# Sharing one pass over the index-query columns between the two halves of 64 tokens

## The chip, the cores and the metric

The kernel runs on one core of one Trainium2 chip. Its time is the device time of one execution in microseconds (us); a lower time is better. The core has a matrix engine (TensorE, PE in the rows; its weight loads are PEld), a vector engine (VectorE, DVE), a scalar engine (ScalarE, ACT), GpSimd (POOL) and a queue engine (SyncE, SP), which issues the transfers from memory here.

## The reference, cut to what matters

One decoder layer on 256 tokens with a model width of 4096. A modulated RMS norm makes `h`, one large projection makes `z`, and two head groups read parts of `z`:

```
mod = silu(c) @ w_ada + b_ada
shift, scale, gate = split(mod, 3)
h = rms_norm(x, norm_g) * (1 + scale) + shift          # 256 x 4096
z = h @ w_in                                           # 4096 x 15520, float32
uA, vA, gA, qB, kB, vB, gB, qI, kI, wI = split(z)
...
dots  = einsum('bqhd,bsd->bqhs', qI, kI)               # lightning indexer, 32 heads of 128
score = einsum('bqh,bqhs->bqs', wI, relu(dots))
score = where(s <= t, score, -inf)
_, sel = top_k(score, 64)                              # k_sel = SEQ / 4
...                                                    # attention over the selected keys
y = concat([yA, yB]) @ w_out
out = x + gate * y
```

`qI` takes 4096 of the 15520 columns of `w_in`, `kI` and `wI` together 160. A query at token t below 64 has at most 64 causal keys, so the top 64 take all of them whatever its scores are: its index queries need not be known.

## The kernel before, in words

**Float32 from three products.** A float32 matrix is split into a rounded part and a rest (`whi` and `wlo` for the weights, `hh` and `hl` for `h`), and `h @ w` is the sum of three products: `hh` with `whi`, `hl` with `whi` and `hh` with `wlo`. ACT writes `whi` (L408), DVE (L414) and POOL (L416) share `wlo`, and PE multiplies in `multiply` (L419 to L437, the matmul at L435). The 128x128 piece of `h` is the stationary operand and a piece of the weights of up to 512 columns streams past it.

**Tiles and blocks.** The unit of the stream is a tile: two rows of 128 of the contraction by up to 512 columns of weights, one transfer of 512 KB. Both token halves (n = 0 for tokens 0 to 127, n = 1 for 128 to 255) are multiplied with it, so a tile has 2 x 3 x 2 = 12 matmuls. The contraction (32 rows of 128) is cut into eight blocks of four. In each block all column groups of the list `early` are visited, two tiles each, and what comes out is added to the groups' sums in SBUF (`add_to`, L800 in the first block, L802 later). That is 46 tiles a block and 368 in all; 128 tiles of the gate columns and 128 of `w_out` follow, 624 in all.

**The head of a block.** The columns of `qI` and of `kI`, `wI` (names `qi0` to `qi7` and `kw`) come first in each block. The 160 columns of `kw` and the 512 of `qi7` are cut as two visits of 336 columns; seven visits of 512 columns follow. These 18 tiles (4 of 336 columns and 14 of 512) are called the head of the block below, the other 28 tiles its tail.

**What runs beside it.** During blocks 0 to 6 the next block's `shift` and `scale` are made on DVE from `w_ada`: 32 steps a block (L196), each with a transfer of 512 KB into one of two buffers `wa`; a step's program asks for the transfer after next (L178). `pace` spreads these steps evenly over the tiles. SP issues all transfers in the order of the program; `raw`, the buffer of a tile's weights, has four places, and a tile's transfer is asked for three tiles ahead (`AHEAD`). `make_h` then makes `hh` and `hl` of the next block, with the float32 `ht` in the pool `s2` (three places). In the last block there are no such transfers; from its eighth tile on the indexer runs between the tiles (`turn` and `weigh`: float32 transposes of `qi` with a reversing matrix `flip`, and float32 products with the keys).

The functions that the change touches and what calls them:

Of the kernel before, what the change touches and what calls it, by code (L numbers as in the profile page):

```python
# [15 lines left out]
P = 128  # L16
# [26 lines left out]
def layer(ctx, tc, x, c, w_ada, b_ada, norm_g, w_in, ln_v_g, ln_v_b, w_s, b_s, q_norm_g,  # L43
# [233 lines left out]
    def modulate(b, md, j, dst):  # L277

        for i in (j, j + 1):
            nc.scalar.activation(dst[:, i - j], xT[b][:, i], AF.Identity, scale=md[:, 1, i:i + 1],  # L280
                                 bias=md[:, 0, i:i + 1])

    def keep_h(b, hh, hl):
        for j in range(BLOCKS[b]):
            h_hi[starts[b] + j] = hh[:, j]
            h_lo[starts[b] + j] = hl[:, j]

    def first_h():
# [26 lines left out]
    def make_h(b, accs):  # L315
# [18 lines left out]
        for j in range(0, nk, 2):  # L334
            nc.gpsimd.tensor_sub(hl[:, j], hts[j // 2][:, 0], hh[:, j].bitcast(F32))
            nc.vector.tensor_sub(hl[:, j + 1], hts[j // 2][:, 1], hh[:, j + 1].bitcast(F32))
            if j + 2 == nk:
                keep_h(b, hh, hl)
            yield
# [40 lines left out]

    def visit(src, parts, ks, c0, w, read, soon=False, before=None):
        v = dict(src=src, parts=parts, ks=ks, c0=c0, w=w, read=read, soon=soon, before=before)
        visits.append(v)
        for i in range(0, len(ks), 2):
            stream.append((v, i))
# [33 lines left out]
    def multiply(t):  # L419

        v, i = stream[t]
        hi, lo = halves.pop(t)
        if i == 0:
            v["ps"] = [mm.tile([P, 512], F32, name="mm_ps", tag="mm") for _ in range(NT)]
        (ah, al), w, n_k = v["parts"], v["w"], len(v["ks"])
        nk = len(hi)
        todo = [(part, kk, n) for kk in range(nk) for part in range(2) for n in range(NT)]
        todo += [(2, kk, n) for kk in range(nk) for n in range(NT)]
        if t + 1 == len(stream):
            todo.sort(key=lambda x: x[2])  # L430
        for part, kk, n in todo:
            k = v["ks"][i + kk]
            a = al if part == 1 else ah
            b = lo if part == 2 else hi
            nc.tensor.matmul(v["ps"][n][:, :w], a[k][:, n * P:(n + 1) * P], b[kk][:, :w],  # L435
                             start=(i + kk == 0 and part == 0),
                             stop=(i + kk == n_k - 1 and part == 2))  # L437

    reads = []

    def step(t):
        load_w(t + AHEAD)
        due = [v for u, v in reads if u <= t]
        del reads[:len(due)]
        for v in due:
            if v["soon"]:
                v["read"](v["ps"])
        split(t)
        flush()
        for v in due:  # L450
            if not v["soon"]:
                v["read"](v["ps"])
        v, i = stream[t]
# [14 lines left out]

    groups["qi7"] = zp.tile([P, NT, 512], F32, name="qi7", tag="qi7")
    groups["kw"] = zp.tile([P, NT, 160], F32, name="kw", tag="kw")  # L470
# [19 lines left out]
    def indexer():  # L490
# [37 lines left out]
        def turn(g, n):  # L528
            tp = misc()
            for hh in range(4):  # L530
                nc.tensor.transpose(tp[:, hh * P:(hh + 1) * P], groups[f"qi{g}"][:, n, hh * P:(hh + 1) * P],
                                    flip)
            box = []

            def read():
                box.append(s2.tile([P, 512], F32, name="qit", tag="s2"))
                nc.scalar.activation(box[0], tp, AF.Copy)
            after(read)
            return box

        def weigh(g, n, qt):
            S = P * (n + 1)
            per = 512 // S
            for h0 in range(0, 4, per):
                dots = misc()
                for a in range(per):
                    nc.tensor.matmul(dots[:, a * S:(a + 1) * S], qt[:, (h0 + a) * P:(h0 + a + 1) * P],
                                     kiT[:, :S], start=True, stop=True)

                def read(dots=dots, h0=h0):  # L550
                    r = s2.tile([P, 512], F32, name="rel", tag="s2")
                    nc.scalar.activation(r, dots, AF.Relu)
                    for a in range(per):
                        hd = g * 4 + h0 + a
                        ws = wi[:, n, hd:hd + 1]
                        if hd == 28:
                            nc.vector.tensor_scalar(score[n], r[:, :S], ws, None, op0=OP.mult)
                        else:
                            nc.vector.scalar_tensor_tensor(score[n], r[:, a * S:(a + 1) * S], ws, score[n],
                                                           op0=OP.mult, op1=OP.add)  # L560
                after(read)

        for g in [7] + list(range(7)):
            for n in range(NT):
# [22 lines left out]
    def attend():  # L587
        mask, score = ix["mask"], ix["score"]

        def choose():  # L590
            for n in range(NT):
                S = P * (n + 1)
                sc = score[n]
                m = mask[:, :P] if n == 0 else mask[:, P:]
                nc.gpsimd.affine_select(sc, sc, pattern=[[-1, S]], compare_op=OP.is_ge, fill=FILL,
                                        base=n * P + P - 1, channel_multiplier=-1)
                yield
                mx = small([P, 8], f"mx{n}")
# [7 lines left out]
                yield  # L606
                nc.gpsimd.affine_select(m, m, pattern=[[-1, S]], compare_op=OP.is_ge, fill=NEG,
                                        base=n * P + P - 1, channel_multiplier=-1)
# [197 lines left out]
    for b, nk in enumerate(BLOCKS):  # L806
        for c0, w, parts in early:
            visit(w_in_t, (h_hi, h_lo), list(range(starts[b], starts[b] + nk)), c0, w, add_to(parts, b == 0),
                  soon=0 < b and nk == 2)
    n_early = len(stream)  # L810


    def mix(g):
# [12 lines left out]
        after(lambda: nc.vector.tensor_mul(wT, tp.rearrange("p (h t) -> p h t", h=4),  # L826
                                           keep[:, None, :].to_broadcast([P, 4, P])))
        yield
        for h0 in range(0, 4, 2):
# [77 lines left out]
    def make_gate(i):  # L907
# [7 lines left out]
        nc.vector.tensor_add(fl[0:1], fl[0:1], ada_tiles.pop(0)[0:1, 0, 0])  # L915
        load_ada()
        for a in range(2):
            hi = s2.tile([P, 512], F32R, name="ghi", tag="s2")
# [13 lines left out]

    GATE_STEPS = 4 * 36

# [142 lines left out]
```

## Time and profile before

| | |
|---|---|
| time, median of 3 runs | 1887.4 us (1884.28 to 1892.18) |
| the profiled execution | 1888.63 us, span from first to last instruction 1886.9 us |
| mean granted TensorE clock | 0.996 |
| PE busy | 1824.8 us, 97% of the span |
| DVE busy | 1447.4 us, 77% |
| POOL busy | 1295.3 us, 69% |
| ACT busy | 933.8 us, 49% |
| moved by transfers | 542.58 MB, mean 288 GB/s |

Busy time is the time in which an engine had at least one instruction under way. PE's matmuls overlap, so its busy share says that it nearly always had one, not how fast they went; the pace is read from the distance of starts. The DMA share is the time that packets took on the core's 16 DMA engines, as a share of their time; it can come out a little over 1.00 in a short stretch.

### The profile page before, as it was taken

To read this page: it belongs to the slowest core of one execution; us is meant where nothing else is said; L and a number is where in the kernel's file an instruction comes from. 1 tells how busy PE (TensorE), PEld (TensorE's weight loads), DVE (VectorE), ACT (ScalarE), POOL (GpSimd) and SP (SyncE) were. 2 spreads that over 40 slices of the span, in tenths; PEclk is the share of its full clock that TensorE was granted. 3 is DMA by queue.
4 is the path that set the end of the run, shared out by engine and by line. 5 is a ranking of instruction groups with operands and counts; after the bars stand their busy time and mean duration, and the time that the engine had idled before them with its cause. 6 is when DMAs were issued, how large, how long until landed. Compare 5 with 4: busy or idle time off the path is not lost. (4 is left out here: it accounts for less than half of the span.)

```text
span 1886.9 us, 27998 instructions
## 1 busy us (share of the span) xinstructions
PE 1824.8 (97%) x8324; PEld 1490.3 (79%) x8324; DVE 1447.4 (77%) x1762; ACT 933.8 (49%) x1737; POOL 1295.3 (69%) x1339
## 2 busy tenths in 40 slices
PE   5799999999999999999999999999999999999998
PEld 2487878878888888788888777787888888888887
DVE  4666888888888888888777898877777677677754
ACT  4356545344453454444445556566654554444443
POOL 0366777777777777777675546766567777877786
PEclk9899999999999999999999999999999999999999
DMA  9999998999989989999874477876789799899964
GB/s 311 339 338 340 332 322 304 331 316 306 335 304 322 321 300 324 328 309 340 284 207 146 128 224 262 272 257 202 242 281 312 248 323 338 295 307 350 334 212 156
DMA packets 269554, 542.58 MB, mean 288 GB/s; under 512 B 17270, under 2 KB 29784, under 8 KB 269404
## 3 DMA queue, kind: packets, MB, share of 16 engines
q1 hardware_dynamic: 269404, 540.79, 84.6%
q8 instruction: 68, 1.11, 0.2%
q14 instruction: 82, 0.67, 0.1%
HBM read 536.51 MB, written 4.22 MB: 287 GB/s over the span
## 5 line engine op out<-in xcount | busy, mean ns | idle before, releaser
L416 POOL TENSOR_TENSOR wlo<-raw,whi 128x512 fp32r<-128x512 f32 (+1 forms) x1248 | 1220.3, 1004 | 536.9 <-ACT whi L408 448.2
L408 ACT ACTIVATE whi<-raw 128x512 fp32r<-128x512 f32 (+1 forms) x1248 | 730.9, 619 | 834.9 <-DMA raw<-in_w_in_dram 407.5
L414 DVE TENSOR_TENSOR wlo<-raw,whi 128x320 fp32r<-128x320 f32 (+2 forms) x624 | 640.7, 1028 | 323.2 <-ACT whi L408 209.4
L435 PE MATMUL mm_ps<-whi,hh 128*128 128x512 f32 (+1 forms) x1984 | 620.4, 394 | 11.4 <-ACT whi L408 9.4
L435 PE MATMUL mm_ps<-whi,hl 128*128 128x512 f32 (+1 forms) x1984 | 604.9, 386 | 2.4 <-DVE hl L303 2.4
L435 PE MATMUL mm_ps<-wlo,hh 128*128 128x512 f32 (+1 forms) x1984 | 525.4, 386 | 5.7 <-DVE wlo L414 4.1
L196 DVE SCALAR_TENSOR_TENSOR acc<-wa,csil,acc 128x1024 f32<-128x1024 f32 x341 | 436.3, 1279 | 57.1 <-DMA wa<-in_w_ada_dram 56.4
L435 PEld LDWEIGHTS mm_ps<-wlo,hh 128*128 128x128 f32 x1984 | 368.9, 188 | 83.8 <-POOL wlo L416 8.8
L435 PEld LDWEIGHTS mm_ps<-whi,hh 128*128 128x128 f32 x1984 | 363.5, 189 | 90.2 <-ACT whi L408 19.9
L435 PEld LDWEIGHTS mm_ps<-whi,hl 128*128 128x128 f32 x1984 | 371.2, 188 | 77.3 <-DVE hl L303 2.9
L435 PE MATMUL mm_ps<-whi,yh 128*128 128x512 f32 x512 | 158.2, 390 | 0.0
L435 PE MATMUL mm_ps<-whi,yl 128*128 128x512 f32 x512 | 158.0, 389 | 0.0
L435 PE MATMUL mm_ps<-wlo,yh 128*128 128x512 f32 x512 | 137.5, 390 | 0.2
L435 PEld LDWEIGHTS mm_ps<-wlo,yh 128*128 128x128 f32 x512 | 95.9, 188 | 21.2 <-POOL wlo L416 1.5
L435 PEld LDWEIGHTS mm_ps<-whi,yh 128*128 128x128 f32 x512 | 95.9, 188 | 20.4 <-ACT whi L408 0.4
L435 PEld LDWEIGHTS mm_ps<-whi,yl 128*128 128x128 f32 x512 | 96.1, 188 | 20.0
L802 DVE TENSOR_TENSOR qi<-qi,mm_ps 128x512 f32<-128x512 f32 (+2 forms) x126 | 73.2, 616 | 0.0
L217 PE MATMUL acc<-wa,csil 128*1 128x512 f32 x64 | 28.1, 629 | 13.2 <-DMA wa<-in_w_ada_dram 13.2
L802 DVE TENSOR_TENSOR u<-u,mm_ps 128x512 f32<-128x512 f32 x56 | 35.6, 675 | 0.0
L802 DVE TENSOR_TENSOR v<-v,mm_ps 128x512 f32<-128x512 f32 x56 | 35.6, 675 | 0.0
L802 DVE TENSOR_TENSOR q<-q,mm_ps 128x512 f32<-128x512 f32 x56 | 35.6, 675 | 0.0
L222 DVE SCALAR_TENSOR_TENSOR accs<-wa,csil,accs 128x1024 f32<-128x1024 f32 x15 | 19.2, 1283 | 17.9 <-DMA wa<-in_w_ada_dram 17.8
(173 smaller groups left out, 797.2 us busy)
## 6 DMA issues: line engine op xcount, KB each, us to landing
raw<-in_w_in_dram SPq DMA_DIRECT2D x464, 512.0 KB, 5.9
wa<-in_w_ada_dram SPq DMA_DIRECT2D x384, 512.0 KB, 5.1
raw<-in_w_out_dram SPq DMA_DIRECT2D x128, 512.0 KB, 6.0
raw<-in_w_in_dram SPq DMA_DIRECT2D x32, 336.0 KB, 4.8
xs<-in_x_dram SPq DMA_DIRECT2D x8, 512.0 KB, 5.4
xres<-in_x_dram SPq DMA_DIRECT2D x8, 512.0 KB, 6.8
out_dram<-yt SPq DMA_DIRECT2D x16, 256.0 KB, 3.6
wk<-rb_d SPq DMA_DIRECT2D x16, 128.0 KB, 4.7
```

The lines of the kernel that those rows point to most:

```text
L196: nc.vector.scalar_tensor_tensor(dst, src, csil[:, k:k + 1], dst, op0=OP.mult, op1=OP.add)
L217: nc.tensor.matmul(acc[g:g + 1, s, :w], csil[:, k:k + 1], wt[:, s], start=i < 4, stop=i >= KC // 2 - 4)
L222: nc.vector.scalar_tensor_tensor(accs, wt, csil[:, k:k + 1], accs, op0=OP.mult, op1=OP.add)
L408: nc.scalar.activation(hi[kk][:, :w], raw[:, kk, :w], AF.Copy)
L414: nc.vector.tensor_sub(lo[kk][:, :cut], raw[:, kk, :cut], hi[kk][:, :cut].bitcast(F32))
L416: nc.gpsimd.tensor_sub(lo[kk][:, cut:w], raw[:, kk, cut:w], hi[kk][:, cut:w].bitcast(F32))
L435: nc.tensor.matmul(v["ps"][n][:, :w], a[k][:, n * P:(n + 1) * P], b[kk][:, :w], start=(i + kk == 0 and part == 0), stop=(i + kk == n_k - 1 ...
L802: nc.vector.tensor_add(z, z, p)
```

## The change

For the columns of `qI` the two halves of `h` of tokens 64 to 127 are laid side by side as one stationary operand of 128 columns (`both`: 64 tokens of the rounded part, 64 of the rest), and tokens 0 to 63 are left out. For n = 0 such a tile needs two products (`both` with `whi`, `both` with `wlo`) in place of three; it also takes along the product of rest with rest. A packed tile so has 10 matmuls in place of 12. The two halves of the sum are added later, in `turn`, by a product with `fold`, which reverses and adds in one (a float32 matmul of 64 columns in place of a transpose of 128). `weigh` and `choose` then work on 64 rows for n = 0. Visits of `kw` stay unpacked, since keys of all tokens are needed: so the 160 columns are a visit of their own, and `qi7` becomes a packed visit of 512 like the others. The head of a block is then 2 tiles of 160 columns and 16 packed tiles of 512, again 18 tiles and the same bytes. `both` is a tile of the pool `s2`, made once a block by two copies on ACT and two subtractions on DVE. `mixes` and `make_gate` get one more step each.

```
+    def side_by_side(b, hts):
+        both = s2.tile([P, BLOCKS[b], 2, 64], F32R, name="both", tag="s2")
+        for i, ht in enumerate(hts):
+            j = slice(2 * i, 2 * i + 2)
+            nc.scalar.activation(both[:, j, 0], ht[:, :, 64:P], AF.Copy)
+            nc.vector.tensor_sub(both[:, j, 1], ht[:, :, 64:P], both[:, j, 0].bitcast(F32))
+        for j in range(BLOCKS[b]):
+            h_both[starts[b] + j] = both[:, j].rearrange("p a b -> p (a b)")
...
-        todo = [(part, kk, n) for kk in range(nk) for part in range(2) for n in range(NT)]
-        todo += [(2, kk, n) for kk in range(nk) for n in range(NT)]
+        for k, b in zip(ks, hi):
+            if v["packed"]:
+                todo += [(0, h_both[k], b), (1, half(ah, k, 1), b), (1, half(al, k, 1), b)]
+            else:
+                todo += [(n, half(a, k, n), b) for a in (ah, al) for n in range(NT)]
+        for k, b in zip(ks, lo):
+            todo += [(n, h_both[k] if v["packed"] and n == 0 else half(ah, k, n), b) for n in range(NT)]
...
-    early.append((O_KW - 176, 336, [("qi7", 336, 176), ("kw", 0, 160)]))
-    early.append((O_KW - 512, 336, [("qi7", 0, 336)]))
-    for g in range(7):
+    add_group("kw", O_KW, 160)
+    for g in range(8):
         add_group(f"qi{g}", O_QI + 512 * g, 512)
...
+        fold = cp.tile([P, 64], F32, name="fold")
+        nc.vector.tensor_add(fold, flip[:, :64], flip[:, 64:])
...
+            q = 64 * (n + 1)
...
+                if n:
+                    nc.tensor.transpose(tp[:, hh * P:(hh + 1) * P], z, flip)
+                else:
+                    nc.tensor.matmul(tp[:, hh * q:(hh + 1) * q], z, fold, start=True, stop=True)
...
-                    nc.tensor.matmul(dots[:, a * S:(a + 1) * S], qt[:, (h0 + a) * P:(h0 + a + 1) * P],
+                    nc.tensor.matmul(dots[:q, a * S:(a + 1) * S], qt[:, (h0 + a) * q:(h0 + a + 1) * q],
                                      kiT[:, :S], start=True, stop=True)
...
-    GATE_STEPS = 4 * 36
+    GATE_STEPS = 4 * 37
...
-        mixed = later(24, mixes(), 20)
+        mixed = later(28, mixes(), 21)
```

On PE the first tile of block 0 stood like this; `hh_437` and `hl_442` are the parts of block 0's `h`, and `x2` and `x4` count the token halves and, for `wlo`, the two rows of weights too:

```order
L435 MATMUL mm_ps<-whi,hh_437 128x336 x2
L435 MATMUL mm_ps<-whi,hl_442 128x336 x2
L435 MATMUL mm_ps<-whi,hh_437 128x336 x2
L435 MATMUL mm_ps<-whi,hl_442 128x336 x2
L435 MATMUL mm_ps<-wlo,hh_437 128x336 x4
```

In the changed program the second tile of `kw` ends and the first packed tile follows like this:

```order
L455 MATMUL mm_ps<-whi,hl_442 128x160 x2
L455 MATMUL mm_ps<-wlo,hh_437 128x160 x4
L455 MATMUL mm_ps<-whi,both 128x512
L455 MATMUL mm_ps<-whi,hh_437 128x512
L455 MATMUL mm_ps<-whi,hl_442 128x512
L455 MATMUL mm_ps<-whi,both 128x512
L455 MATMUL mm_ps<-whi,hh_437 128x512
L455 MATMUL mm_ps<-whi,hl_442 128x512
L455 MATMUL mm_ps<-wlo,both 128x512
L455 MATMUL mm_ps<-wlo,hh_437 128x512
L455 MATMUL mm_ps<-wlo,both 128x512
L455 MATMUL mm_ps<-wlo,hh_437 128x512
```

A tile of 336 columns has 12 matmuls, as one of 512 had, and so has one of 160; a packed tile has 10.

On PE in the last block, the first `turn` of the indexer, the tile behind it and the first `weigh` stood like this:

```order
L531 MATMUL ms_ps<-flip,qi_166 128x128 x4
L435 MATMUL mm_ps<-whi,hh_9195 128x512 x2
L435 MATMUL mm_ps<-whi,hl_9306 128x512 x2
L435 MATMUL mm_ps<-whi,hh_9195 128x512 x2
L435 MATMUL mm_ps<-whi,hl_9306 128x512 x2
L435 MATMUL mm_ps<-wlo,hh_9195 128x512 x4
L547 MATMUL ms_ps<-ix,qit 128x128 x4
```

In the changed program the same place reads like this (`fold` in place of `flip`; `ix` holds the keys, `qit` the turned queries):

```order
L554 MATMUL ms_ps<-fold,qi_167 128x64 x4
L455 MATMUL mm_ps<-whi,both 128x512
L455 MATMUL mm_ps<-whi,hh_8992 128x512
L455 MATMUL mm_ps<-whi,hl_9103 128x512
L455 MATMUL mm_ps<-whi,both 128x512
L455 MATMUL mm_ps<-whi,hh_8992 128x512
L455 MATMUL mm_ps<-whi,hl_9103 128x512
L455 MATMUL mm_ps<-wlo,both 128x512
L455 MATMUL mm_ps<-wlo,hh_8992 128x512
L455 MATMUL mm_ps<-wlo,both 128x512
L455 MATMUL mm_ps<-wlo,hh_8992 128x512
L571 MATMUL ms_ps<-ix,qit 64x128 x4
```

The transposes became float32 matmuls of half the columns, and the product with the keys gives 64 rows in place of 128.

On SP at the border of block 0 and block 1 the transfers stood like this:

```order
L396 DMA raw<-in_w_in_dram 128x2x512
L396 DMA raw<-in_w_in_dram 128x2x336
L178 DMA wa<-in_w_ada_dram 128x2x512
L396 DMA raw<-in_w_in_dram 128x2x336
L178 DMA wa<-in_w_ada_dram 128x2x512
L396 DMA raw<-in_w_in_dram 128x2x336
L178 DMA wa<-in_w_ada_dram 128x2x512
L396 DMA raw<-in_w_in_dram 128x2x336
```

In the changed program they stand like this:

```order
L409 DMA raw<-in_w_in_dram 128x2x160
L178 DMA wa<-in_w_ada_dram 128x2x512
L409 DMA raw<-in_w_in_dram 128x2x160
L178 DMA wa<-in_w_ada_dram 128x2x512
L409 DMA raw<-in_w_in_dram 128x2x512
L178 DMA wa<-in_w_ada_dram 128x2x512
L409 DMA raw<-in_w_in_dram 128x2x512 x2
```

Two small transfers take the place of two of four middling ones; those of `w_ada` keep their places among the tiles.

## Rows read from the trace of the kernel before

**Rows 1.** The page: busy us (share of the span) xcount of each engine.

```profile
PE 1824.8 (97%) x8324; PEld 1490.3 (79%) x8324; DVE 1447.4 (77%) x1762; ACT 933.8 (49%) x1737; POOL 1295.3 (69%) x1339
```

**Rows 2.** Waits of the whole span: who waited for whom, us, times, longest.

```profile
ACT whi L408 <- DMA raw<-in_w_in_dram: 407.5, 198, 37.2
...
PEld mm_ps L435 <- ACT whi L408: 20.3, 29, 1.9
```

**Rows 3.** Timeline of PE in block 6's tail: start, us, what, count.

```profile
903.64 1.07 PE L435 MATMUL mm_ps<-wlo,hh 128*128 128x512 f32 x4
...
906.36 1.07 PE L435 MATMUL mm_ps<-wlo,hh 128*128 128x512 f32 x4
```

**Rows 4.** Timeline of PE where block 6 begins: four tiles of 336 columns.

```profile
836.11 0.47 PE L435 MATMUL mm_ps<-whi,hh 128*128 128x336 f32 x2
...
843.47 0.62 PE L435 MATMUL mm_ps<-whi,hh 128*128 128x512 f32 x2
```

**Rows 5.** Windows, heads of blocks 0-7: length, engines' busy us, PE clock, DMA share, GB/s.

```profile
70.33:121.64 51.31, 48.88 (x217) 41.87 (x217) 34.29 (x38) 28.41 (x55) 32.71 (x34) 0.91 0.92 321
202.64:248.96 46.32, 46.10 (x218) 38.74 (x217) 39.46 (x49) 20.11 (x37) 35.15 (x37) 1.00 0.96 335
328.28:375.99 47.71, 46.10 (x218) 38.69 (x216) 39.91 (x50) 19.01 (x34) 33.85 (x35) 1.00 0.95 325
455.58:503.52 47.94, 46.23 (x217) 38.76 (x216) 41.56 (x51) 19.11 (x34) 34.67 (x36) 1.00 0.95 329
581.76:629.27 47.51, 46.81 (x217) 38.71 (x216) 41.87 (x52) 19.80 (x36) 34.65 (x36) 1.00 0.95 327
709.18:756.61 47.43, 46.46 (x218) 38.89 (x216) 40.81 (x52) 19.33 (x35) 34.98 (x37) 1.00 0.94 329
836.11:882.79 46.68, 45.81 (x218) 38.81 (x216) 40.81 (x51) 20.17 (x36) 35.42 (x37) 1.00 0.97 334
961.45:1013.97 52.52, 52.52 (x266) 44.33 (x264) 38.87 (x54) 26.34 (x43) 33.66 (x37) 1.00 0.62 185
```

**Rows 6.** Windows of 10 us: at the start, and in block 0; columns as above.

```profile
50.00:60.00 10.00, 7.51 (x16) 1.00 (x16) 4.85 (x5) 0.00 (x0) 0.00 (x0) 1.00 1.05 399
110.00:120.00 10.00, 10.00 (x46) 8.29 (x45) 5.51 (x7) 5.31 (x11) 5.67 (x7) 1.00 1.00 348
```

**Rows 7.** Timeline of PE in block 7's head, where the indexer runs between tiles.

```profile
989.07 0.53 PE L522 MATMUL ms_ps<-kw,flip 128*128 128x32 f32 x4
989.44 0.70 PE L435 MATMUL mm_ps<-whi,hh 128*128 128x512 f32 x2
...
992.64 0.71 PE L435 MATMUL mm_ps<-whi,hh 128*128 128x512 f32 x2
...
995.48 1.05 PE L547 MATMUL ms_ps<-ix,qit 128*128 128x128 f32 x8
996.29 0.71 PE L435 MATMUL mm_ps<-whi,hh 128*128 128x512 f32 x2
...
999.47 0.71 PE L435 MATMUL mm_ps<-whi,hh 128*128 128x512 f32 x2
...
1002.32 1.89 PE L547 MATMUL ms_ps<-ix,qit 128*128 128x256 f32 x8
1003.85 0.58 PE L435 MATMUL mm_ps<-whi,hh 128*128 128x512 f32 x1
```

**Rows 8.** Timeline of all engines in block 3's head; in brackets the idle time before.

```profile
469.85 1.17 DVE L414 TENSOR_TENSOR wlo<-raw,whi 128x320 fp32r<-128x320 f32 x1
...
473.29 0.48 DVE L414 TENSOR_TENSOR wlo<-raw,whi 128x320 fp32r<-128x320 f32 x1
...
475.69 1.28 DVE L196 SCALAR_TENSOR_TENSOR acc<-wa,csil,acc 128x1024 f32<-128x1024 f32 x1
...
478.22 1.27 DVE L802 TENSOR_TENSOR qi<-qi,mm_ps 128x512 f32<-128x512 f32 x2
```

**Rows 9.** Waits of SP, which issues the transfers, from 212 to 944 us.

```profile
SPq L178 <- DVE acc L196: 270.3, 136, 3.9
```

More of the change, by code (lines that the diff above doesn't have):

```diff
@@ L337, in make_h @@
             if j + 2 == nk:
+                h_both.clear()
+                side_by_side(b, hts)
                 keep_h(b, hh, hl)
@@ L379, in layer, with visit @@
     stream = []
-    def visit(src, parts, ks, c0, w, read, soon=False, before=None):
-        v = dict(src=src, parts=parts, ks=ks, c0=c0, w=w, read=read, soon=soon, before=before)
+    def visit(src, parts, ks, c0, w, read, packed=False, before=None):
+        v = dict(src=src, parts=parts, ks=ks, c0=c0, w=w, read=read, packed=packed, before=before)
         visits.append(v)
@@ L424, in multiply, with half @@
             v["ps"] = [mm.tile([P, 512], F32, name="mm_ps", tag="mm") for _ in range(NT)]
-        (ah, al), w, n_k = v["parts"], v["w"], len(v["ks"])
-        nk = len(hi)
-        todo = [(part, kk, n) for kk in range(nk) for part in range(2) for n in range(NT)]
-        todo += [(2, kk, n) for kk in range(nk) for n in range(NT)]
-        if t + 1 == len(stream):
[L430 to L437, printed above, removed]
+        (ah, al), w, ks = v["parts"], v["w"], v["ks"][i:i + len(hi)]
+        def half(a, k, n):
+            return a[k][:, n * P:(n + 1) * P]
+        todo = []
+        for k, b in zip(ks, hi):
[5 more added lines that the diff above has]
+            todo += [(n, h_both[k] if v["packed"] and n == 0 else half(ah, k, n), b) for n in range(NT)]
+        if t + 1 == len(stream):
+            todo.sort(key=lambda x: x[0])
+        ends = {n: max(j for j, x in enumerate(todo) if x[0] == n) for n in range(NT)}
+        begun = set() if i == 0 else {0, 1}
+        for j, (n, a, b) in enumerate(todo):
+            nc.tensor.matmul(v["ps"][n][:, :w], a, b[:, :w], start=n not in begun,
+                             stop=i + len(hi) == len(v["ks"]) and j == ends[n])
+            begun.add(n)
     reads = []
@@ L444, in step @@
         del reads[:len(due)]
-        for v in due:
-            if v["soon"]:
-                v["read"](v["ps"])
         split(t)
@@ L450, in step @@
         for v in due:
-            if not v["soon"]:
-                v["read"](v["ps"])
+            v["read"](v["ps"])
         v, i = stream[t]
@@ L542, in weigh @@
             S = P * (n + 1)
+            q = 64 * (n + 1)
             per = 512 // S
+            sc = score[n][:q]
             for h0 in range(0, 4, per):
@@ L551, in read @@
                     r = s2.tile([P, 512], F32, name="rel", tag="s2")
-                    nc.scalar.activation(r, dots, AF.Relu)
+                    nc.scalar.activation(r[:q], dots[:q], AF.Relu)
                     for a in range(per):
                         hd = g * 4 + h0 + a
-                        ws = wi[:, n, hd:hd + 1]
-                        if hd == 28:
-                            nc.vector.tensor_scalar(score[n], r[:, :S], ws, None, op0=OP.mult)
+                        ws = wi[:q, n, hd:hd + 1]
+                        if hd == 0:
+                            nc.vector.tensor_scalar(sc, r[:q, :S], ws, None, op0=OP.mult)
                         else:
-                            nc.vector.scalar_tensor_tensor(score[n], r[:, a * S:(a + 1) * S], ws, score[n],
+                            nc.vector.scalar_tensor_tensor(sc, r[:q, a * S:(a + 1) * S], ws, sc,
                                                            op0=OP.mult, op1=OP.add)
                 after(read)
-        for g in [7] + list(range(7)):
+        for g in range(8):
             for n in range(NT):
@@ L808, in layer @@
             visit(w_in_t, (h_hi, h_lo), list(range(starts[b], starts[b] + nk)), c0, w, add_to(parts, b == 0),
-                  soon=0 < b and nk == 2)
+                  packed=parts[0][0].startswith("qi"))
     n_early = len(stream)
```

23 lines of the change are left out of this document (13 added, 10 removed).

## The prediction

> **What bounds the kernel now.** The page comes first: PE had a matmul under way 97% of the time, DVE 77%, POOL 69%, ACT 49% [rows 1]. Such a share doesn't tell the pace, so the next view is PE's timeline. In an undisturbed stretch a tile of 512 columns starts 2.72 us after the one before [rows 3], 0.2267 us for each of its 12 matmuls. Where block 6 begins, four tiles of 336 columns take 7.36 us [rows 4]: 1.84 us each, 0.153 us a matmul. A head (18 tiles) would so take 4 x 1.84 + 14 x 2.72 = 45.4 us if PE alone set its length. The windows show more: in blocks 1 to 6 the heads last 46.3 to 47.9 us, in the mean 47.3 [rows 5], 1.9 us over PE's need.
>
> The waits say what fills these 1.9 us. ACT stood idle 407 us in all for weights that hadn't landed, and PE's weight loads 20 us for ACT [rows 2]: ACT needs a tile's weights, PE needs ACT, and mostly the weights come just in time. The windows say why: in the heads of blocks 1 to 6 the transfers are at a share of 0.94 to 0.97 and 325 to 335 GB/s [rows 5], since the next block's `w_ada` comes beside `w_in`. Two resources are nearly full there: PE needs 45.4 us of 47.3, the transfers 47.3 x 0.953 (the mean share) = 45.1 us. In the head of block 7 no `w_ada` is read for modulation, the share is 0.62, and PE is busy all of the 52.5 us [rows 5]: there PE alone sets the time. This difference decides what a shorter tile is worth.
>
> **What the change removes.** A packed tile has 10 matmuls: 10 x 0.2267 = 2.27 us, 0.45 us less than 2.72. Seven visits of two tiles become packed in each block: 14 x 0.453 = 6.3 us of PE's need. The four tiles of 336 columns (7.36 us) become two packed ones (4.53 us) and two of 160 columns with 12 matmuls each.
>
> **The 160 columns.** No row shows this float32r matmul with so few columns. From below: the line through 512 and 336 columns (0.2267 and 0.153 us) gives 0.080 us at 160, but the four passes of 32 columns at 989.07 took 0.37 us, 0.0925 us each [rows 7], so a pass doesn't get shorter than that here; a tile takes 12 x 0.0925 = 1.1 us. From above: a plain float32 product, which runs as two passes (four in the program stand as x8). From 992.64 to 996.29 a tile and eight passes of 128 columns take 3.65 us, so a pass takes (3.65 - 2.72) / 8 = 0.116 us; from 999.47 to 1003.85 it is (4.38 - 2.72) / 8 = 0.2075 us for 256 columns [rows 7]. At 160 that makes 0.139 us, for two passes 0.278 us, and 3.3 us a tile. I take 1.1 us, because the 336-column row is of the same type and kernel line; 3.3 us is the second rival.
>
> The Trainium skill (TensorE: Matmul & The Clock Gate, LDWEIGHTS) gives a weight load the time of its columns at 1.2 GHz, 107 ns for 128, which would make the 160-column tile 1.28 us by estimate and the sum 0.4 us worse in block 7. The row of 32 columns, 92.5 ns, is below that, so the measurement decides against it here.
>
> **Heads of blocks 1 to 6.** PE's need falls to 2 x 1.1 + 16 x 2.27 = 38.5 us (42.9 with 3.3 us tiles). The bytes are the same, 4 x 336 = 2 x 160 + 2 x 512 columns, and `w_ada` is paced by tiles, of which there are still 18. So the transfers need their 45.1 us at a share of 1.00, and they now are the longer need. A share of 1.00 with 348 GB/s is in the trace for 10 us of block 0; at the start a share of 1.05 with 399 GB/s is seen, which would make it 42.9 us [rows 6]. I take 45.1, because the first of these rows is of this very work: 47.3 - 45.1 = 2.2 us a block. The bounds are 1.1 (half of the saving goes to the same irregular arrivals that cost 1.9 us today) and 4.4. Six blocks: 13.2 us (6.6 to 26). Most of the 6.3 us that PE saves in a block is so given back as waiting for weights.
>
> **Block 0.** Its head is at 0.92, with PE waiting for `hl` and at a clock of 0.91 in the mean [rows 5], and its last part at 1.00 [rows 6]: between 0 and 51.3 x 0.08 = 4 us; I take 1.5, nearer to nothing, since `pace` must bring the first 33 steps into 37 tiles.
>
> **Block 7.** PE's need counts in full: -6.3 us for 14 tiles, and 7.36 - 4.53 - 2.2 = 0.6 us for the four others. Against it stands `fold`: 4 float32 products are 8 passes of at least 0.0925 us, 0.74 us, at most 8 x 0.116 = 0.93 us. The four transposes take 3.20 - 2.72 = 0.48 us now (989.44 to 992.64) [rows 7]. That is 0.26 to 0.45 us more for each of eight `turn`s, 2.1 to 3.6 us; I take 2.8, the middle. `weigh` for n = 0 streams the same 128 columns: nothing. Together -4.1 us; with the 3.3 us tile about 0.
>
> **What I count at nothing.** `both` costs two copies on ACT and two subtractions of 128 columns on DVE per block. They run in the tail of the block before, where later blocks' PE work covers them; ACT is busy 20 of 47 us [rows 5]. Without cover they cost up to 2 x 1.17 us on DVE (the 320-column row [rows 8]). The subtractions wait for the copies, and behind them on DVE stands the next `wlo`; the copies follow a `whi` directly, so little waits. `both` holds one of three `s2` places until the last packed tile. In block 7 `rel` then waits for another place, with the next `whi` behind it on ACT; five or six such steps at up to 1.28 us (one DVE instruction, [rows 8]) would be 7 us. I take 0, because PE gates that stretch and DVE is busy 38.9 of 52.5 us there [rows 5]. The extra steps in `mixes` and `make_gate` spread the same work over the same tiles.
>
> **Sum.** 13.2 + 1.5 + 4.1 = 18.8 us. The profiled execution took 1888.6 us, 1.2 over the median of 1887.4: 1888.6 - 18.8 = 1869.8. I forecast 1870 us; with the bounds this case spans 1855 to 1878.
>
> **Rivals.**
> *PE sets the pace everywhere.* If transfers can go faster once they are asked for earlier, a head takes 38.5 + 1.9 = 40.4 us: 6 x 6.9 + 4 + 4.1 = 49 us less, 1839 us. That needs 47.3 us x 330 GB/s in 40.4 us, 386 GB/s. For it: 399 GB/s for 10 us at the start. Against it: 348 at a share of 1.00 in block 0 [rows 6].
> The Trainium skill (HBM Reference, Specifications) says that a core that streams alone gets some 425 GB/s; by that rule this rival would hold. The trace's row at a share of 1.00 doesn't agree, and its best row stays below.
>
> *The 160-column tile takes 3.3 us.* PE then needs 42.9 us a head beside the transfers' 45.1; two needs so near each other add waits as today, so I count the half, 1.1 us a block: 6.6 + 0.5 + 0 = 7 us, 1881.5 us. For it: the float32 rows [rows 7]. Against it: the line of the float32r rows.
>
> *Slower: DVE sets a packed tile's length.* DVE works in order: 1.17 us `wlo`, 0.64 us of adds (1.27 us for two tiles), 1.28 us of L196 in 32 of 46 tiles, 0.89 [rows 8]: 2.70 us a tile, as long as a tile today. SP waits 270 us for L196 before it can ask for more, with the next weights queued behind [rows 9]. A head of 16 x 2.70 + 2 x 3.3 = 49.8 us is 2.5 over today; in seven blocks 17.5, in all 1906 us. It decides from a 160-column tile of (47.3 - 43.2) / 2 = 2.05 us on. Against it: `wlo` takes only 0.48 us at other times [rows 8], and DVE is busy 39.5 to 41.9 us in these heads [rows 5], 2.3 us a tile.
>
> *Nothing gained in blocks 0 to 6*, because the loads' chain holds at today's pace: 1884 us.
>
> **How the numbers follow.** The forecast gets 0.45, PE's pace 0.13, the slow 160 columns 0.27, DVE 0.08, nothing gained 0.07. The range 1848 to 1884 holds the forecast, nearly all of the second rival and a little of the first and of the last: about 0.78 to 0.8. A measurement here can tell about 0.5% from no change, 9.4 us: faster means under 1878.0, slower over 1896.8. Faster: 0.42 of the forecast, 0.13, and 0.10 of the slow-160 case, 0.65. Slower: 0.08. Same: the remaining 0.27.
>
> **What the next profile would show.** Right: in the heads of blocks 1 to 6 a DMA share near 1.00, length near 45 us, PE with more idle time before `whi`; undisturbed packed tiles 2.27 us apart in block 7. Wrong: heads of 40 to 42 us with over 370 GB/s (then PE is still the bound), or 160-column tiles of 3 us, or heads at 47 us with a DMA share of 0.95 and DVE without gaps.

## The result, and the profile after

| | before | after |
|---|---|---|
| time, median | 1888.4 us (1884.3 to 1895.5, 7 runs) | 1899.8 us (1896.7 to 1909.0, 7 runs) |
| the profiled execution, and its span | 1888.6 us, 1886.9 us | 1899.8 us, 1898.0 us |
| mean granted TensorE clock | 0.996 | 0.991 |

The ratio is 1.0063, with a 95% interval of 1.0039 to 1.0087: the changed kernel is 0.6% slower, where 1870 us had been forecast and 1884 was the end of the range. The page of the changed kernel says that the work did shrink; this line answers to [rows 1]:

```profile
PE 1808.0 (95%) x8100; PEld 1444.8 (76%) x8100; DVE 1467.7 (77%) x1765; ACT 937.4 (49%) x1751; POOL 1305.1 (69%) x1340
```

PE has 224 matmuls less and was busy 17 us less, but the span grew by 11.1 us: PE is idle 28 us more. To see where, I cut both traces at the starts of PE's tiles:

| stretch, us | before | after | difference |
|---|---|---|---|
| start of block 0 | 70.3 | 69.3 | -1.0 |
| block 0 | 132.3 | 131.0 | -1.3 |
| heads of blocks 1 to 6, mean | 47.27 | 48.29 | 6 x +1.02 |
| tails of blocks 1 to 6, mean | 79.20 | 80.60 | 6 x +1.40 |
| block 7 (head, tail) | 52.52, 106.87 | 47.59, 110.18 | -1.6 |
| gate columns and output, to PE's last matmul | 761.3 | 761.7 | +0.4 |

The sum is +11.0 us. Nearly all of the loss lies in blocks 1 to 6, 14.5 us, in heads as in tails. Block 2's tail before and after (columns as in [rows 5]):

```profile
375.99:455.58 79.59, 79.00 (x354) 64.53 (x353) 67.96 (x82) 37.94 (x67) 60.13 (x61) 1.00 0.91 309
...
376.81:458.26 81.45, 80.02 (x353) 64.25 (x352) 69.14 (x84) 36.98 (x69) 59.12 (x61) 1.00 0.90 300
```

The windows of the heads of blocks 0 to 7 of the changed kernel (columns as in [rows 5], to which these rows answer):

```profile
69.34:120.19 50.85, 45.72 (x184) 35.68 (x185) 35.46 (x39) 29.34 (x55) 33.64 (x34) 0.89 0.92 315
200.38:250.25 49.87, 43.83 (x185) 30.98 (x184) 39.51 (x47) 20.65 (x36) 34.27 (x35) 1.00 0.94 320
330.24:376.81 46.57, 43.66 (x185) 32.58 (x184) 38.74 (x47) 19.64 (x34) 34.30 (x35) 0.96 0.95 325
458.26:507.58 49.32, 44.41 (x185) 34.36 (x184) 40.27 (x49) 19.71 (x34) 34.67 (x36) 0.93 0.94 321
587.81:636.65 48.84, 43.05 (x185) 32.77 (x184) 41.19 (x51) 20.16 (x36) 34.83 (x36) 0.97 0.94 321
716.85:764.42 47.57, 42.81 (x186) 33.03 (x184) 40.88 (x48) 19.61 (x34) 34.20 (x35) 0.96 0.95 323
846.28:893.82 47.54, 42.03 (x186) 31.85 (x184) 40.59 (x50) 19.59 (x34) 34.84 (x35) 1.00 0.97 336
973.66:1021.25 47.59, 47.59 (x241) 38.89 (x240) 36.80 (x53) 26.30 (x43) 34.40 (x37) 1.00 0.68 204
```

The column to read first is the last but one, the DMA share: 0.94 to 0.97 in blocks 1 to 6, where it was 0.94 to 0.97 before [rows 5]. PE now asks for weights earlier, and the transfers have not become any fuller. PE is idle 2.9 to 6.0 us in each of these heads (length less busy time), where it was idle 0.2 to 1.7 us. In block 7, where PE sets the time, the head fell by 4.9 us as its share of 0.68 allows.

Who waits for whom in the whole span (before, these four were 407.5, 20.3, 9.4 and 10.3 us; the first two stand in [rows 2]):

```profile
ACT whi L421 <- DMA raw<-in_w_in_dram: 401.3, 184, 34.7
...
PEld mm_ps L455 <- ACT whi L421: 55.3, 55, 2.7
...
PE mm_ps L455 <- ACT whi L421: 34.4, 38, 2.4
PEld mm_ps L455 <- POOL wlo L429: 30.5, 56, 3.4
```

ACT itself waits for the weights' transfer, in all as long as before; what grew is PE's waiting for ACT and for POOL. SP, which issues that transfer, waits as before [rows 9] for a sum of the modulation on DVE. SP's waits from 212 to 960 us:

```profile
SPq L178 <- DVE acc L196: 288.2, 145, 5.1
SPq L178 <- DMA wa<-in_w_ada_dram: 94.9, 82, 3.7
```

The timeline in block 6's head shows what this wait does (start, length, engine, line, what; DVE's L196 is the sum, SPq's L178 the transfer of `w_ada`, L409 that of a tile's weights):

```profile
860.46 1.28 DVE L196 SCALAR_TENSOR_TENSOR acc<-wa,csil,acc 128x1024 f32<-128x1024 f32 x1
...
861.77 0.37 SPq L178 DMA_DIRECT2D wa<-in_w_ada_dram  x1
...
862.23 0.42 SPq L409 DMA_DIRECT2D raw<-in_w_in_dram  x1
...
863.64 1.29 DVE L196 SCALAR_TENSOR_TENSOR acc<-wa,csil,acc 128x1024 f32<-128x1024 f32 x1 [0.68 <-DMA wa<-in_w_ada_dram]
...
864.96 0.37 SPq L178 DMA_DIRECT2D wa<-in_w_ada_dram  x1
...
865.42 0.93 SPq L409 DMA_DIRECT2D raw<-in_w_in_dram  x2
```

A sum ends at 861.74 (860.46 and 1.28); 0.03 us later SP issues the next `wa`, because the buffer has come free, and 0.46 us after that the weights of a tile, which stood behind it in the program. The same happens at 864.93, 864.96 and 865.42. The places for these weights had been free for about 2 us (POOL's `wlo` of the tiles that held them had ended at 859.8 and 863.4); the weights were queued behind a transfer that waited for DVE.

**The theory.** This order closes a loop. The weights asked for at 865.42 land 7.3 us later (ACT's `whi` of that tile starts at 872.71 after 3.78 us of waiting); then `whi` takes 0.6 us until DVE can begin, `wlo` 1.17, adds up to 1.27, the next sum 1.29, and only then SP goes on. `raw` has four places, so one round trip carries four tiles. Other weights of this head land 5 to 8 us after their issue; the mean from issue to `whi` over the 108 tiles of the heads of blocks 1 to 6 is 6.4 us. With that mean and the 4.3 us of the four steps a trip takes 10.7 us, 2.7 us a tile and 48 us a head of 18 tiles (an estimate from these rows; with 5 and with 8 us it would be 42 and 55), whatever PE needs. The rivals: the packed tiles simply run into the transfers' rate; the loss is that of the two tiles of 160 columns, which PE uses up in 1.3 us each; or DVE is too busy in a head (the slower rival of the prediction).

### The profile page after: what moved, and what is told of

Same layout as the page of the kernel before. It is cut to its first block, busy times and chain, and to the rows that moved or that the text cites. A ratio compares the mean times of both kernels' runs of the same rounds, so it can differ in the third digit from the quotient of the medians.

```text
span 1898.0 us, 27567 instructions
## 1 busy us (share of the span) xinstructions
PE 1808.0 (95%) x8100; PEld 1444.8 (76%) x8100; DVE 1467.7 (77%) x1765; ACT 937.4 (49%) x1751; POOL 1305.1 (69%) x1340
## 5 line engine op out<-in xcount | busy, mean ns | idle before, releaser
L455 PE MATMUL mm_ps<-whi,hh 128*128 128x512 f32 (+1 forms) x1728 | 566.1, 397 | 9.4 <-ACT whi L421 8.0
L455 PE MATMUL mm_ps<-whi,hl 128*128 128x512 f32 (+1 forms) x1728 | 552.7, 389 | 2.7 <-DVE hl L313 2.7
L196 DVE SCALAR_TENSOR_TENSOR acc<-wa,csil,acc 128x1024 f32<-128x1024 f32 x341 | 436.3, 1280 | 52.8 <-DMA wa<-in_w_ada_dram 52.0
L455 PEld LDWEIGHTS mm_ps<-whi,hh 128*128 128x128 f32 x1728 | 318.0, 190 | 82.0 <-ACT whi L421 18.0
L455 PEld LDWEIGHTS mm_ps<-wlo,hh 128*128 128x128 f32 x1728 | 322.3, 190 | 75.8 <-POOL wlo L429 9.5
L455 PEld LDWEIGHTS mm_ps<-whi,hl 128*128 128x128 f32 x1728 | 324.9, 190 | 70.4 <-DVE hl L313 2.9
L455 PE MATMUL mm_ps<-whi,both 128*128 128x512 f32 x256 | 106.6, 416 | 26.6 <-ACT whi L421 26.4
L455 PE MATMUL mm_ps<-wlo,both 128*128 128x512 f32 x256 | 106.1, 414 | 5.6 <-DVE wlo L427 3.7
L455 PEld LDWEIGHTS mm_ps<-whi,both 128*128 128x128 f32 x256 | 49.5, 193 | 47.6 <-ACT whi L421 36.8
L455 PEld LDWEIGHTS mm_ps<-wlo,both 128*128 128x128 f32 x256 | 49.2, 192 | 35.2 <-POOL wlo L429 19.3
L829 DVE TENSOR_TENSOR qi<-qi,mm_ps 128x512 f32<-128x512 f32 x112 | 71.2, 674 | 0.0
```

The lines of the kernel that those rows point to most:

```text
L196: nc.vector.scalar_tensor_tensor(dst, src, csil[:, k:k + 1], dst, op0=OP.mult, op1=OP.add)
L455: nc.tensor.matmul(v["ps"][n][:, :w], a, b[:, :w], start=n not in begun, stop=i + len(hi) == len(v["ks"]) and j == ends[n])
L829: nc.vector.tensor_add(z, z, p)
```

## The experiments

**The two small tiles alone.** The kernel before, with its columns cut as in the change and nothing packed:

```
...
-    early.append((O_KW - 176, 336, [("qi7", 336, 176), ("kw", 0, 160)]))
-    early.append((O_KW - 512, 336, [("qi7", 0, 336)]))
-    for g in range(7):
+    add_group("kw", O_KW, 160)
+    for g in range(8):
...
```

> The kernel before with one part of the change alone: the 160 columns are a visit of their own and qi7 a visit of 512 columns, all tiles with 12 matmuls. Theory 1 (two small transfers leave too few bytes on the way, so PE runs dry behind them): PE saves nothing that matters (2 x 1.30 + 2 x 2.72 in place of 7.36 us, +0.7 us a head), but tiles 1 to 3 of a block take 3 us and more as in the changed kernel, heads of blocks 1 to 6 get 1 to 2 us longer than 47.3, in all 6 to 14 us slower. Rival (the small tiles are harmless, the packed tiles bring the loss): heads at 47 to 48 us, within 4 us of before.

Measured: 1896.95 us, ratio to before 1.0037 (1.0016 to 1.0058). In the profiled run blocks 1 to 6 last 759.2 us, as before (758.8); the heads are 47.72 and the tails 78.81 us in the mean. PE runs out of weights behind the small tiles (the second and third tile of a block last up to 4.4 us) and catches up later. So the cut by itself costs some tenths of a per cent, and in this trace not in blocks 1 to 6 but at block 0 (+1.1), block 7 (+1.9) and behind (+2.8).

**Packed, without the small tiles.** The changed kernel with `kw` and the last index head as one unpacked visit of 288 columns and a packed one of 384:

```
-    add_group("kw", O_KW, 160)
-    for g in range(8):
...
+    early.append((O_KW - 128, 288, [("qi7", 384, 128), ("kw", 0, 160)]))
+    early.append((O_KW - 512, 384, [("qi7", 0, 384)]))
+    for g in range(7):
...
```

> The changed kernel, but the 160 columns go with the last index head (a visit of 288 columns with 12 matmuls), and the other three heads of qi7 are a packed visit of 384 columns; bytes of a head are the same, and no tile is as small as 160. Theory 1 (small tiles leave too few bytes on the way): tiles 1 to 3 lose their stalls, heads of blocks 1 to 6 fall from 48.3 to 46 or 47 us, 7 to 14 us faster than the changed kernel. Rival (packed tiles run into the loads wherever the columns are cut): heads stay at 48 us, within 3 us of the changed kernel.

Measured: 1896.51 us, ratio 1.0033 (1.0015 to 1.0050). Heads 47.30, tails 80.79 us. The kernel is still slower than before and its heads still take 47 us, so the small tiles are at most a part, some 3 us by the medians, of the loss.

**No transfers of `w_ada` in blocks 0 to 6.** The changed kernel; its sums on DVE stay and read what lies in the buffers, and the modulation of blocks 1 to 7 is left out in that sense:

```
...
+            if ns == 2 and len(reuse) == 2:
+                ada_tiles.append(reuse[len(ada_loads) % 2])
+                return
...
```

> The changed kernel without the transfers of w_ada for blocks 1 to 7 (all but the first two of them; DVE's sums run on what these two brought, so shift and scale of these blocks are not the reference's). Theory 2 (the transfers' rate or their place in SP's queue sets the heads): heads of blocks 1 to 6 fall to PE's need, 39 to 41 us, and tails to 78 us, in all some 60 us less than the changed kernel. Rival (DVE's work sets them): heads stay at 46 to 48 us.

Measured: 1826.05 us in one run. The windows of block 3's head and tail (columns as above):

```profile
427.99:466.94 38.95, 38.95 (x186) 32.73 (x184) 37.51 (x49) 22.56 (x36) 35.53 (x37) 1.00 0.81 237
466.94:544.95 78.01, 78.01 (x354) 64.89 (x353) 66.99 (x83) 39.32 (x67) 59.40 (x59) 1.00 0.63 183
```

The head is 38.95 us, PE without a gap: 2 x 1.31 + 16 x 2.27 us. DVE is busy 37.5 of these 38.95 us with all of its sums and delays nobody. So neither DVE's load nor the small tiles hold the heads at 48 us; the transfers do, by their rate or by their order.

**Transfers whole, sums small.** The changed kernel; after the first step a sum takes 8 of 1024 columns, the rest of the modulation's sums is left out:

```
-                    nc.vector.scalar_tensor_tensor(dst, src, csil[:, k:k + 1], dst,
-                                                   op0=OP.mult, op1=OP.add)
+                    few = 8 if ns == 2 else 1024
+                    nc.vector.scalar_tensor_tensor(dst[:, :few], src[:, :few], csil[:, k:k + 1],
+                                                   dst[:, :few], op0=OP.mult, op1=OP.add)
```

> The changed kernel with all transfers, but the sums of w_ada for blocks 1 to 7 take 8 of 1024 columns after the first step (so shift and scale of these blocks are not the reference's). DVE's 1.28 us per step become some 0.1 us. If the transfers' rate sets the heads: 45 to 48 us as in the changed kernel, share of the transfers at 0.95 to 1.0. If it is the chain (SP waits for a sum on DVE before it asks for the next weights, which stand behind in its queue): heads fall to 42 to 44 us with more GB/s than 336. If DVE's work itself sets them: 39 to 41 us.

Measured: 1858.03 us in one run; heads 43.06, tails 78.36 us. The windows of the heads of blocks 1 and 5:

```profile
199.95:242.53 42.58, 40.53 (x186) 32.09 (x184) 27.89 (x45) 20.55 (x36) 34.75 (x35) 1.00 1.00 360
686.01:729.02 43.01, 41.72 (x185) 31.37 (x184) 29.81 (x47) 19.14 (x34) 33.90 (x34) 1.00 0.98 347
```

The same transfers now pass at a share of 0.97 to 1.00 and the head is 5.2 us shorter. The transfers' rate was not the bound of the changed kernel; DVE's sum in the loop was. What is left over 38.95 us is put down to the transfers here because of this share; the paced runs at the end, with fewer bytes in a head, bear it out.

**The loop cut, everything computed.** The transfer of `w_ada` is issued behind the weights' transfer of the same step, in the changed kernel and, as a control, in the kernel before:

```
-            load_ada()
+            behind.append(load_ada) if ns == 2 else load_ada()
...
         load_w(t + AHEAD)
+        while behind:
+            behind.pop(0)()
```

> The changed kernel with one thing moved: in blocks 0 to 6 the next transfer of w_ada stands on SP behind the weights asked for in the same step, not ahead of them; the same transfers, the same instructions elsewhere. Theory (chain: a tile's weights are asked for only when a sum on DVE is done, 1.28 us and the adds later than their buffer is free, and this loop over four tiles takes 2.6 us a tile whatever PE needs): heads of blocks 1 to 6 fall from 48.3 to 43 to 45 us, tails from 80.6 to 79, in all 20 to 35 us faster than the changed kernel and 10 to 20 us faster than the kernel before. Rival (the rate of the transfers is full at a share of 0.95): heads at 47 to 48 us, within 5 us of the changed kernel.

> The same move in the kernel before. If the chain also sets the heads of the kernel before (47.3 us where PE needs 45.4): heads fall to 45.4 to 46 us and tails to 78.5, 8 to 17 us faster than before. If before was bound by PE and only the changed kernel by the chain: within 4 us of before.

Measured: 1864.48 us, ratio 0.9861 (0.9840 to 0.9881), and for the kernel before with this order 1874.97 us, ratio 0.9920 (0.9900 to 0.9939). SP's wait for the sum in the changed kernel fell from 288 to 81 us:

```profile
SPq L179 <- DVE acc L197: 81.3, 68, 3.7
```

SP still waits, but for something else: the waits put down to `wlo` on DVE rose from 114 to 360 us, since SP now mostly waits until a place of `raw` is free. The loop shows more directly in the time by which the weights' issue lies behind the last read of the place that they go to, in the mean over the 108 tiles of the heads of blocks 1 to 6. It was 1.36 us before and 1.41 us after the change, 0.59 us with small sums, and 0.09 and 0.08 us with the late transfer in the changed kernel and in the kernel before.

The windows of the heads of blocks 1, 3 and 5 and of block 5's tail, in the changed kernel with the late transfer:

```profile
201.28:244.75 43.47, 40.63 (x186) 32.07 (x184) 34.28 (x45) 20.19 (x36) 32.10 (x34) 1.00 1.00 357
444.48:487.75 43.27, 41.48 (x185) 33.59 (x184) 35.13 (x48) 20.54 (x35) 32.75 (x35) 0.96 1.00 358
688.71:732.08 43.37, 40.08 (x186) 32.18 (x184) 35.25 (x47) 20.29 (x35) 33.80 (x36) 1.00 1.01 363
...
732.08:810.72 78.64, 78.61 (x354) 64.87 (x354) 68.62 (x85) 39.52 (x69) 57.56 (x59) 1.00 0.91 310
```

And block 3's head of the kernel before with it:

```profile
450.95:496.87 45.92, 45.88 (x217) 38.77 (x216) 37.02 (x51) 21.16 (x36) 33.91 (x37) 1.00 0.97 337
```

Two things follow. The kernel before had the loop too: without it its heads fall from 47.3 to 45.85 us, where PE has no gap and needs 45.4. And with the loop gone the change does what it was to do: heads of 43.8 us at a share of 1.00, tails of 78.7 us, 10.5 us (0.6%) less in all than the kernel before with the same order. The sign of the change depends on the place of one transfer in the queue.

**`both` on GpSimd.** Are the tails longer because of `both`'s subtractions on DVE?

```
-            nc.vector.tensor_sub(both[:, j, 1], ht[:, :, 64:P], both[:, j, 0].bitcast(F32))
+            nc.gpsimd.tensor_sub(both[:, j, 1], ht[:, :, 64:P], both[:, j, 0].bitcast(F32))
```

> The changed kernel with the two subtractions that make `both` on POOL in place of DVE. If they are what makes the tails longer (80.6 against 79.2 us), tails of blocks 1 to 6 fall by 1 us or more, 6 to 9 us in all; if the tails are longer because the head ends without weights in hand, they stay within 0.5 us and the time within 4 us of the changed kernel.

Measured: 1894.70 us, ratio 1.0024 (1.0004 to 1.0044); tails 80.55 us, as in the changed kernel (80.60). DVE's part of `both` is not the reason for the tails. The median is 5 us under the changed kernel's, more than the 4 us expected; the profiled run, at 1904.2 us the slowest of the twelve, doesn't tell where these lie. With the loop cut the tails are 78.7 us with `both` on DVE.

**128 rows in the products with the keys.** The changed kernel; for n = 0 these products get 128 columns of the stationary operand again, of which 64 rows are used:

```
                 nc.scalar.activation(box[0][:, :4 * q], tp[:, :4 * q], AF.Copy)
+                if not n:
+                    nc.scalar.activation(box[0][:, 256:320], tp[:, 192:256], AF.Copy)
...
-                    nc.tensor.matmul(dots[:q, a * S:(a + 1) * S], qt[:, (h0 + a) * q:(h0 + a + 1) * q],
+                    nc.tensor.matmul(dots[:, a * S:(a + 1) * S], qt[:, (h0 + a) * q:(h0 + a) * q + P],
```

> The changed kernel with 128 columns of stationary operand in the products with the keys for n = 0, as before (the 64 columns of the next head ride along and their rows are not read; one more small copy on ACT per turn). The tiles of block 7 beside such a product take 3.96 us in the changed kernel and 3.66 before. If 64 output rows are what costs, these tiles go back to 3.66 and block 7 gets 2 to 3 us shorter (157.8 us in the changed kernel); if not, 3.96 and no change. Tiles beside `turn` with fold stay at 3.73 either way.

Measured: 1885.97 us in one run, 14 us under the changed kernel. First PE's timeline in block 7's head of the changed kernel:

```profile
1000.68 1.00 PE L554 MATMUL ms_ps<-fold,qi 128*128 128x64 f32 x8
1001.49 0.48 PE L455 MATMUL mm_ps<-whi,both 128*128 128x512 f32 x1
...
1003.65 0.40 PE L455 MATMUL mm_ps<-wlo,hh 128*128 128x512 f32 x1
1003.98 1.09 PE L571 MATMUL ms_ps<-ix,qit 128*64 128x128 f32 x8
1005.00 0.50 PE L455 MATMUL mm_ps<-whi,both 128*128 128x512 f32 x1
```

And the same place with 128 rows:

```profile
1005.22 0.39 PE L455 MATMUL mm_ps<-wlo,hh 128*128 128x512 f32 x1
1005.46 1.05 PE L573 MATMUL ms_ps<-ix,qit 128*128 128x128 f32 x8
1006.26 0.48 PE L455 MATMUL mm_ps<-whi,both 128*128 128x512 f32 x1
```

With 64 rows the next tile starts 1.02 us after the first product, with 128 rows 0.80, and the product itself starts 0.33 and 0.24 us after the matmul ahead: 0.31 us more, 2.5 us for eight of them. Block 7 went from 157.8 to 155.0 us. The rest of the 14 us between the two runs lies in blocks 0 to 6, which this edit doesn't touch (764.6 in place of 773.3 us in blocks 1 to 6). One run doesn't tell whether that is more than scatter, and why stays open.

**The best of these, and the transfers' bound.** Late transfer and 128 rows together; then, besides, the steps of the modulation paced slower in the heads and so faster in the tails, where the share is 0.91 to 0.94 in blocks 1 to 5:

```
-                     for b in range(1, len(BLOCKS)) if (KC + 1) * b > steps] + [0.0])
+                     for b in range(1, len(BLOCKS)) if (KC + 1) * b > steps] + [0.0]) * (0.8 if t % 46 < 18 else 1.0)
```

> The changed kernel with two edits together that were each tried alone: the transfer of w_ada is put behind the weights' transfer of its step, and the products with the keys for n = 0 have 128 output rows again. If the two add up: the late transfer alone gave 1864.5 us, and the eight products take 8 x 0.30 = 2.4 us less in block 7, so 1862 us. Rival: block 7 is no longer at PE's pace with the later order, and the 0.30 us each come back as waits there: 1864 to 1865 us.

> As the kernel before in this call, and the modulation's steps are paced at 0.8 of their rate in the heads, so that 11 in place of 13 fall into a head of blocks 1 to 6 and 22 in place of 20 into its tail. Theory (with the chain cut, the transfers are the bound of the heads: share 1.00, 357 to 363 GB/s): two steps are 1.05 MB less, 2.9 us at 360 GB/s; heads fall from 43.8 to about 41 us, and the tails, at a share of 0.91 to 0.94, have room for 13 GB/s more and keep 78 to 78.7 us: six times 2.9 = 17 us less, about 1845 us. Rival (what holds the heads at 43.8 is still a wait for another engine, not the transfers' rate): heads stay at 43 to 44 us and the time at 1861 us.

> The same at 0.6 of the rate: 8 steps in a head, 25 in a tail. Theory: heads reach PE's need, 39 us, 4.8 us less; but the tails' transfers go from about 314 to 347 GB/s, a share of 1.01, and DVE there from 67 to 73 of 78 us, so the tails get longer by 1 to 3 us: net 2 to 4 us a block, 1840 to 1850 us, the same as at 0.8 or a little better. Rival (waits for another engine hold the heads): heads at 43 us or over, tails longer by 1 to 3 us, 1865 to 1875 us.

Measured, against before at 1890.0 us:

| | time, us | ratio (95%) | heads, tails, block 0 |
|---|---|---|---|
| late, 128 rows | 1862.9 (1855.0 to 1866.7) | 0.9852 (0.9829 to 0.9876) | 44.33, 78.33, 132.6 |
| and steps at 0.8 in heads | 1853.8 (1851.1 to 1859.6) | 0.9808 (0.9787 to 0.9829) | 41.41, 79.86, 136.3 |
| and steps at 0.6 in heads | 1865.7 (1862.8 to 1871.6) | 0.9875 (0.9856 to 0.9895) | 40.11, 81.32, 144.1 |

Block 4's head and tail at 0.8:

```profile
567.91:608.73 40.82, 39.72 (x185) 32.48 (x184) 37.49 (x46) 21.22 (x36) 35.13 (x36) 1.00 1.01 361
608.73:688.98 80.25, 79.37 (x353) 64.53 (x352) 66.62 (x86) 38.01 (x67) 58.20 (x60) 1.00 0.93 318
```

And at 0.6 block 0's tail and block 4's head:

```profile
578.66:618.52 39.86, 39.29 (x186) 32.59 (x184) 35.95 (x43) 19.92 (x34) 35.24 (x36) 1.00 0.98 338
116.70:214.24 97.54, 85.94 (x354) 68.54 (x352) 61.70 (x64) 53.13 (x97) 55.95 (x59) 0.93 0.89 296
```

Late transfer and 128 rows together are 1.6 us under the late transfer alone, less than the scatter of these runs, so it is not shown that the two add up. Some two transfers fewer in a head (10.3 in place of 12 in the mean) make it 2.9 us shorter, as the theory said, 17.5 us in six. But I had taken the tails to have room, and they don't: each got 1.5 us longer, and block 0 3.7 us, which takes 12.9 us back. The medians differ by 9.1 us, where 17 were expected; the traced run of the version with 0.8 was its slowest. At 0.6 the heads are within 1.2 us of PE's need and the tails, block 0's above all (97.5 us, PE idle 11.6 of them), take back more than that. The version with 0.8 is the fastest of those that compute everything, 1.9% under the kernel before.

## Why the prediction was wrong

**What held.** A packed tile takes 2.27 us as worked out, PE's need in a head fell to 38.95 us (38.5 predicted), and a tile of 160 columns took 1.30 us (1.1 taken, 3.3 the upper bound), so the second rival is out. Block 0 gave 1.3 us (1.5 taken), but that is within the scatter, so luck: in the near-equal programs of the experiments (even tiles, `both` on GpSimd, 128 rows) it lasted 127.3 to 134.5 us. The slower rival, DVE as the pace of a packed tile, falls with the run without `w_ada` transfers: DVE had all its sums, and the heads were at PE's need. Of the last sign of being wrong, heads of 47 us at a share of 0.95 came, but DVE had gaps of 6.7 to 10.4 us in each head.

**The step that failed** is in the heads of blocks 1 to 6: "PE needs 45.4 us of 47.3, the transfers 47.3 x 0.953 (the mean share) = 45.1 us", and from it "the transfers need their 45.1 us at a share of 1.00, and they now are the longer need". A head at a share of 0.953 was read as a transfer system 95% used that would fill up once PE let it. But a transfer that hasn't been issued can't fill it. The heads were held at 47 to 48 us by the loop through SP's queue, and the row for it stood among the evidence: SP waits for the sum with "the next weights queued behind" [rows 9]. I used that row for DVE as a pace, and gave the case in which "the loads' chain holds at today's pace" 0.07. It holds in four variants: heads of 47.3 (before), 47.7 (cut alone), 47.3 (even) and 48.3 us (after). 13.2 of the forecast 18.8 us are lost with that step.

The number itself was not bad. With the loop cut, by a late transfer or by small sums, the heads come to 43.8 and 43.1 us at shares of 0.97 to 1.01 and 347 to 363 GB/s: the transfers' bound is there, a little lower than 45.1.

The prediction set the Trainium skill's 425 GB/s for one core (HBM Reference, Specifications) against a row of 348. Another place in the Trainium skill (DMA: Bandwidth & Descriptors, Where 436 GB/s comes from) gives some 358 GB/s as what binds transfers from HBM; the heads with the late transfer at a share of 1.00 and 1.01 lie near that, with 356 to 363 GB/s over 43 us. It is no hard bound here: over a single head of 39 us a run had 373.

**Why slower, and not the same.** "Nothing gained" was put at 1884 us; 16 us more were measured. They lie in three places: 2.5 us in block 7, 8.4 in the tails and 6.1 in the heads, less 1 to 2 us elsewhere. *Block 7* was to give 4.1 us and gave 1.6. `fold` makes a `turn` 0.45 us longer (a tile of 12 matmuls with one lasts 3.73 in place of 3.28 us), which is the upper bound: 8 x 0.45 = 3.6 us where 2.8 were taken. The line "`weigh` for n = 0 streams the same 128 columns: nothing" is wrong by 0.31 us for each of eight, 2.5 us. With 2 x 0.2 us for the tiles of 160 columns, block 7 would by these terms have gained only 0.4 us. Of the other 1.2 us, 0.7 are no gain: four transposes of `wsr` that lay in the block's last tile (3.60 us, now 2.92) come one tile later, behind the block. Where the other 0.5 come from is open. *The tails* were not in the sum at all: 6 x 1.4 = 8.4 us. A head that ends with no weights in hand passes its waits on: by the starts of PE's tiles, 0.95 of these 1.40 us lie in the first seven of the 28 tiles. The rest may be the loop in the tail itself, since `w_ada` is read there too; how much each took is not settled. Both ways of cutting the loop bring the tails back to 78.4 to 78.7 us. *The heads* lost 6.1 us against before. From 200 to 960 us PE now has nine idle times of 1.6 to 2.4 us, where the kernel before has none over 1.5 us and a granted clock of 1.00 in all these heads [rows 5]. With five of the nine the granted clock fell to 0.50 for some matmuls. In block 3 (timeline, in brackets the idle time):

```profile
485.91 2.39 ACT L421 ACTIVATE whi<-raw 128x512 fp32r<-128x512 f32 x4 [4.07 <-DMA raw<-in_w_in_dram]
...
486.59 0.54 PE L455 MATMUL mm_ps<-whi,both 128*128 128x512 f32 x1 [2.31 <-ACT whi L421]
...
486.93 0.63 PE L455 MATMUL mm_ps<-whi,hh 128*128 128x512 f32 x1
...
487.35 0.63 PE L455 MATMUL mm_ps<-whi,hl 128*128 128x512 f32 x1
```

And the windows of that place:

```profile
486.93:490.33 3.40, 3.40 (x9) 2.67 (x8) 3.15 (x5) 1.83 (x5) 3.40 (x4) 0.50 0.97 330
490.57:493.00 2.43, 2.43 (x12) 2.02 (x11) 2.43 (x3) 1.06 (x3) 2.24 (x3) 1.00 0.79 255
```

ACT had waited 4.07 us for weights and PE 2.31 us for ACT; then the granted clock is 0.50, 1.2 in place of 2.4 GHz, and eight matmuls start 0.42 us apart in place of 0.23, 1.6 us in all. The five lie in the heads of blocks 2 to 5: at most 8 us, since part of it lies where PE would have waited anyway. How the 6.1 us divide between these, the small tiles and chance is not settled: near-equal programs (even tiles, `both` on GpSimd, 128 rows) had heads of 47.3 to 47.5 us and one or two such stretches.

## What to carry to other kernels

Before a saving is booked against "the transfers' share at 1.00", ask why the share is under 1.00 now: if the queue that issues the transfers waits for an engine, with the transfers that matter behind it, the stretch is a loop whose round trip sets the time, and a faster engine outside the trip gains nothing in it. In a queue that issues in order, put the transfer that may wait (a buffer freed late) behind the one that is needed first; here that is worth 0.8% to the old kernel, and against the kernel of the same order it turns the change from 0.6% slower to 0.6% faster (1.4% with both). And a stretch that ends without anything in hand passes its waits on to the next, so the next stretch belongs into the sum.

## What the runs showed of the hardware that was not expected

- Four float32 products (eight passes) with 64 output rows took 0.3 us more than four with 128 rows and the same 128 streamed columns (1.02 and 0.80 us, and 0.09 us at their start).
- Matmuls of 160 columns start 0.108 us apart (1.30 us for 12), not 0.0925 as the row of 32 columns had suggested. The Trainium skill's 107 ns for a weight load of 128 columns (TensorE: Matmul & The Clock Gate, LDWEIGHTS), against which the prediction had decided, agrees with it.
- An idle time of PE of 2.3 us, in a stretch at 1.00, was followed by eight matmuls at a granted clock of 0.50. Idle times of 1.6 to 1.9 us in the same run came both with and without such a fall.
